# Grouped-query heads: the triangles of two key tiles share one block up to its transposing, and masks part them before the product with the values

## The chip, the cores and the metric

The kernel runs on one core of a Trainium2 chip. The metric is device time in microseconds (us), of which a smaller value is better. The time before the change is 1879.26 us, the median of three runs (1879.20, 1879.26 and 1881.03). The engines are named as in the profile: PE is the matrix engine (PEld its weight loads), DVE the vector engine, ACT the scalar engine, POOL the GpSimd engine, and SP the engine that issues the DMAs.

## The reference

One block of a transformer, in float32, for 512 positions and a width of 2048: a norm, one input projection whose columns are split over three kinds of mixers (A: 8 heads of dilated attention, B: a convolution module, C: 16 heads of windowed attention), an output projection with its residual, a second norm and a gated feed-forward network. The change concerns C alone: 16 query heads of 64, which share 2 heads of keys and values, with a window of 128 and one learned sink for each head.

```python
# q, k: normalised per head; G = 8 query heads for one key head
s = jnp.einsum('nbqhgd,nbkhd->nbhgqk', qb, kb) * (hd ** -0.5)
dist = qpos[:, :, None] - kpos[:, None, :]
valid = (dist >= 0) & (dist <= max_dist) & (kpos[:, None, :] >= 0)      # max_dist = 127
s = jnp.where(valid[None, :, None, None], s, -jnp.inf)
m = jnp.maximum(jnp.max(s, axis=-1), sk)                                # sk: the sink
p = jnp.exp(s - m[..., None])
denom = jnp.sum(p, axis=-1) + jnp.exp(sk - m)
o = jnp.einsum('nbhgqk,nbkhd->nbqhgd', p, vb) / denom
```

The positions form four tiles of 128. Query q of a tile looks at keys 0 to q of its own tile and at keys q+1 to 127 of the tile ahead of it. So the keys that a query may see are two triangles, one in each of two key tiles, and the two triangles together are exactly one square of 128 by 128.

## The kernel before

All products of the projections are made in three parts, from float32 values that are split into a high part (fp32r) and the low remainder. The input projection `project()` goes through 30 column tiles of 128 columns; a column tile is 16 blocks of the width, and a block is three matmuls of 512 columns (L312, L313, L314). After every second block, so after six projection matmuls, `project()` calls `ticks.tick()` (L486). The class `Ticks` (L91) holds a list of steps for each tick: `ticks.after(n, step, ...)` puts a step n ticks ahead, and `tick()` issues what has come due. So the attention steps stand in the instruction streams between groups of six projection matmuls, at places that whole numbers set, and each engine goes through its own stream in that order. The queue is not rearranged by times.

Heads are worked in pairs: a tile of the query projection (cq0 to cq7, worked in the order cq0 cq3 cq1 cq5 cq2 cq7 cq4 cq6) holds two heads. In the names of tiles, c5t is the bank of transposes of tile cq5, and so on; c5s, c5e, c5ph, c5pl and c5o are its scores, its exps, the high and the low part of the transposed weights, and its product with the values. `attention()` queues the steps of one head (`head(h)`), with the distances of the table `C_TICKS` (L43). For a C head they are:

- `scores` (two units, two ticks apart): for query tiles 0 and 1, then 2 and 3, the product of queries with the keys of the own tile and of the tile ahead, 256 columns (for tile 0: 128). PE writes the bank c5s (L736, L738, L739).
- `top`: DVE adds the mask `bias_c` to the scores and takes the maximum of each row (L750), and makes nm, the negative maximum times the row's scale.
- `exps`: ACT makes the exps with their sums: 128 columns for query tile 0, and 256 for each of the others (L763). Masked entries come out as zero.
- `norm`: DVE adds the sink's share and makes the reciprocal, and POOL scales the exps by it (L779), in the same widths: 128 and three times 256.
- `flip`: PE transposes the blocks of 128 by 128 (L795): seven of them for a head, two each for query tiles 1 to 3 and one for tile 0. They lie in two banks by `TBANKS` (L708): four blocks, and three blocks one tick later.
- `high` and `low`, for each bank: ACT casts the transposed block to fp32r (c5ph, L801), and a tick later DVE makes the remainder (c5pl, L806).
- `weigh`: PE multiplies the values with the transposed weights: eight matmuls (L819, L820), high and low in turn, since a key tile serves the query tile of its own and the one behind it: six of 256 columns and two of 128.
- `out_high` and `out_rows`: ACT and DVE gather the result in mix_c5 (L828); its split into mh_c and ml_c (ml_c on POOL, L865) feeds the output projection.

The second head of a pair runs six ticks behind the first, by the table's `every`. The products of the first head are in the same tick as the first transposes of the second.

All buffers of 128 x 512 come from one pool of 67 slots (`slot()`, L145), the banks of PSUM from `bank()`. The mixer A has eight heads with the same steps, but another table (`A_TICKS`); B works on DVE, with 30 taps for each of four tiles (L513), between the same projections.

Of the kernel before, what the change touches and what calls it, by code (L numbers as in the profile page):

```python
# [15 lines left out]
P = 128  # L16
T = 512
# [25 lines left out]
C_TICKS = (1, 6, 2, 2, 2, 2, 4, 1, 3)  # L43
# [79 lines left out]
def kernel(ctx: ExitStack, tc: tile.TileContext, xT, wi, wo, wgu, wd, cst_in, outT):  # L123
# [254 lines left out]
    bias_c = slot("bias_c", cols=2 * P)  # L378
# [5 lines left out]
    nc.gpsimd.iota(di2[:, :2 * P], pattern=[[-1, 2 * P]], base=P, channel_multiplier=1)  # L384
# [294 lines left out]
    def do_v(box, b, name):  # L679
# [29 lines left out]
        "c": [[(0, 0, 1), (1, 1, 2)], [(2, 2, 3), (3, 3, 3)]],  # L709
# [5 lines left out]
    def attention(kind, box, mix, mi, heads):  # L715
# [3 lines left out]
        mask = bias_c if kind == "c" else bias_a  # L719
        mw = mask.shape[-1]  # L720
        st = {}

        def head(h):
# [17 lines left out]
            def top(u):  # L741
                b, rq = banks[u], box["rq"]
                s = slice(us[u][0][0], us[u][-1][0] + 1)
                if kind == "c" and u == 0:
                    with_kl = slot(f"kl{h}", F32, P)
                    nc.scalar.copy(with_kl, b[:, P:2 * P])
                    nc.vector.tensor_add(with_kl, with_kl, mask[:, mw - P:])
                for i, k0, n, o in reversed(us[u]):
                    other = with_kl if kind == "c" and i == 0 else mask[:, mw - n:]
# [7 lines left out]
            def exps(u):  # L757
                b, rq = banks.pop(u), box["rq"]
                e = es[u] = slot(f"{name}e{h}{u}")
                s = slice(us[u][0][0], us[u][-1][0] + 1)  # L760
                for i, k0, n, o in us[u]:
                    acc = dict(accum_out=den[:, i:i + 1]) if kind == "c" else {}
                    nc.scalar.activation(e[:, o:o + n], b[:, o:o + n], AF.Exp, bias=nm[:, i:i + 1],  # L763
                                         scale=rq[:, i, h:h + 1], **acc)
# [3 lines left out]
            def norm(u):  # L768
# [9 lines left out]
                for i, k0, n, o in us[u]:  # L778
                    nc.gpsimd.tensor_scalar(e[:, o:o + n], e[:, o:o + n], rd[:, i:i + 1], None, op0=ALU.mult)  # L779
# [3 lines left out]
            def block(i, j):  # L783
                for u, un in enumerate(us):
# [14 lines left out]
            def high(t, b, o):  # L799
                ph[t] = slot(f"{name}ph{h}{t}", F32R)  # L800
                nc.scalar.copy(ph[t][:, :o], b[:, :o])  # L801
                ticks.after(EV, low, t, b, o)

            def low(t, b, o):
                pl[t] = slot(f"{name}pl{h}{t}", F32R)
                nc.vector.tensor_sub(pl[t][:, :o], b[:, :o], ph[t][:, :o].bitcast(F32))  # L806

            def weigh():
                b = bank(f"{name}o{h}")
                vals = box["v"][h]  # L810
                first = True
                for t, tb in enumerate(TBANKS[kind]):
# [251 lines left out]
    m_hi = m_lo = r1b = mult_a = bias_a = bias_c = None  # L1064
# [471 lines left out]
```

## Time and profile before

| what | us |
|---|---|
| median of three runs | 1879.26 |
| span of the profiled execution | 1877.5 |
| matmuls of the input projection, start of the first to the last | 5 to 397 |
| transposes of the C heads, among them | 136 to 371 |
| matmuls of the output projection | 398 to 593 |
| matmuls of the feed-forward network, from | 593 |

The runs' time holds a little around the span of the profile. A line of a timeline reads: start, duration, engine, line of the kernel, operation, output and inputs by the program's names, and the shape; one line may stand for several instructions that follow each other (x3). A line of groups gives the count, the busy time and the mean of one in ns, and behind a second bar the idle time of the engine ahead of these instructions, with what ended it. "<-DVE c0pl" names the engine and the tile whose result ended a wait. All durations of the profile come from one execution.

### The profile page before, as it was taken

What the parts mean: (1) busy time and instruction counts of PE and PEld (TensorE: products, weight loads), DVE (VectorE), ACT (ScalarE), POOL (GpSimd) and SP (SyncE); (2) the same over time, 40 slices, a digit from 0 to 9 for tenths busy, and PEclk for the clock granted to TensorE, in tenths of its full rate; (3) what the DMA queues carried; (4) which work ended last, traced back from release to release, by engine and by line L of the source; (5) the groups of instructions that cost most, each with busy time, mean ns of one, the idle gap of its engine ahead of it and who ended that gap; (6) DMA issues with size and microseconds to landing.
All of it is one profiled execution on the core that took longest, in us unless ns stands there. A gap on an engine that the chain in (4) does not pass through costs nothing.

```text
span 1877.5 us, 28557 instructions
## 1 busy us (share of the span) xinstructions
PE 1871.7 (100%) x9848; PEld 1609.1 (86%) x9848; DVE 1454.1 (77%) x2376; ACT 1343.7 (72%) x1883; POOL 1217.0 (65%) x812
## 2 busy tenths in 40 slices
PE   9999999999999999999999999999999999999999
PEld 7888888888888888888888888888888888888888
DVE  7578999897679777777777777777777677778887
ACT  6246655553466887888878888888888887777675
POOL 5023444362155887778878877888787767766786
PEclk9999999999999999999999999999999999999999
DMA  7333233333342354443544445344455475578984
GB/s 271 122 109 102 81 105 102 121 107 138 113 146 89 114 178 142 163 163 132 184 134 164 162 137 181 132 166 160 145 175 196 151 237 185 196 253 283 311 241 124
DMA packets 157986, 301.09 MB, mean 160 GB/s; under 512 B 29968, under 2 KB 69008, under 8 KB 157840
## 3 DMA queue, kind: packets, MB, share of 16 engines
q1 hardware_dynamic: 157696, 299.25, 48.8%
q8 instruction: 78, 1.28, 0.3%
q14 instruction: 68, 0.56, 0.1%
q10 hardware_dynamic: 144, 0.01, 0.0%
HBM read 241.27 MB, written 50.33 MB: 155 GB/s over the span
## 4 chain that ended last, share of the span: by engine, by line
PE 96%; DVE 1%; issue 1%; ACT 1%; POOL 1%; DMA 0%; SPq 0%; DVEq 0%; POOLq 0%; ACTq 0%
PE out L1125 51%; PE out L1267 16%; PE o L313 3%; PE o L314 3%; PE o L312 3%; PE cq L312 1%; PE cq L313 1%; PE cq L314 1%; PE in L313 1%; PE ak L312 1%; PE bg L312 1%; PE ak L314 1%; PE ak L313 1%; PE bu L312 1%; PE bu L314 1%; PE bg L313 1%
## 5 line engine op out<-in xcount | busy, mean ns | idle before, releaser
L1125 PE MATMUL out<-h,wh 128*128 128x512 f32 x2464 | 588.4, 391 | 0.0
L1125 PEld LDWEIGHTS out<-h,wh 128*128 128x128 f32 x2464 | 452.7, 188 | 87.5
L1125 PEld LDWEIGHTS out<-h,wl 128*128 128x128 f32 x2464 | 316.2, 191 | 12.4 <-DVE wl L295 0.4
L1125 PE MATMUL out<-h,wl 128*128 128x256 f32 x2464 | 320.3, 283 | 0.2 <-DVE wl L295 0.2
L1267 PE MATMUL out<-wh,a 128*128 128x512 f32 x896 | 221.3, 389 | 0.0
L1267 PEld LDWEIGHTS out<-wh,a 128*128 128x128 f32 x896 | 168.2, 188 | 34.9
L289 ACT CAST wh<-w 128x1024 fp32r<-128x1024 f32 (+1 forms) x93 | 96.7, 1042 | 125.0 <-PE o L313 43.3
L290 DVE TENSOR_TENSOR wl<-w,wh 128x1024 fp32r<-128x1024 f32 (+1 forms) x93 | 117.2, 1262 | 46.7 <-ACT wh L289 45.7
L1267 PE MATMUL out<-wl,a 128*128 128x512 f32 x448 | 119.7, 389 | 0.0
L1267 PEld LDWEIGHTS out<-wl,a 128*128 128x128 f32 x448 | 84.1, 188 | 17.4
L513 DVE SCALAR_TENSOR_TENSOR y<-bu,cst,y 128x511 f32<-128x511 f32 (+14 forms) x120 | 90.3, 753 | 0.7
L1125 PE MATMUL out<-a,wh 128*128 128x512 f32 x330 | 80.1, 391 | 0.0
L1125 PEld LDWEIGHTS out<-a,wh 128*128 128x128 f32 x330 | 60.2, 188 | 11.4
L312 PE MATMUL o<-mh_c,wh 128*128 128x512 f32 x128 | 51.2, 400 | 0.0
L313 PE MATMUL o<-ml_c,wh 128*128 128x512 f32 x128 | 50.1, 392 | 0.4 <-POOL ml_c L865 0.3
L314 PE MATMUL o<-mh_c,wl 128*128 128x512 f32 x128 | 50.1, 391 | 0.0
L1312 DVE TENSOR_TENSOR Y<-Y,out 128x512 f32<-128x512 f32 x48 | 30.8, 683 | 19.0 <-PE out L1267 18.9
L1125 PEld LDWEIGHTS out<-a,wl 128*128 128x128 f32 x330 | 43.3, 191 | 2.2
L1125 PE MATMUL out<-a,wl 128*128 128x256 f32 x330 | 44.0, 283 | 0.0
L429 POOL TENSOR_TENSOR ssum<-ssum,sq 128x512 f32<-128x512 f32 x15 | 26.6, 1770 | 19.3 <-ACT sq L428 18.8
L312 PE MATMUL cq<-hh,wh 128*128 128x512 f32 x96 | 38.6, 402 | 0.0
L314 PE MATMUL cq<-hh,wl 128*128 128x512 f32 x96 | 37.5, 391 | 0.0
(3111 smaller groups left out, 5197.0 us busy)
## 6 DMA issues: line engine op xcount, KB each, us to landing
od<-a SPq DMA_DIRECT2D x140, 256.0 KB, 4.7
a<-od SPq DMA_DIRECT2D x140, 256.0 KB, 6.2
w<-in_wi SPq DMA_DIRECT2D x59, 512.0 KB, 3.6
w<-in_wo SPq DMA_DIRECT2D x32, 512.0 KB, 3.6
x<-in_xT SPq DMA_DIRECT2D x16, 256.0 KB, 6.7
xr<-in_xT SPq DMA_DIRECT2D x16, 256.0 KB, 3.8
x2d<-xr SPq DMA_DIRECT2D x16, 256.0 KB, 2.0
yd<-z SPq DMA_DIRECT2D x16, 256.0 KB, 5.5
```

The lines of the kernel that those rows point to most:

```text
L289: nc.scalar.copy(hi[:, :n], t[:, :n])
L290: eng.tensor_sub(lo[:, :n], t[:, :n], hi[:, :n].bitcast(F32))
L312: nc.tensor.matmul(out, wh, xh, start=start, stop=False)
L313: nc.tensor.matmul(out, wh, xl, start=False, stop=False)
L314: nc.tensor.matmul(out, wl, xh, start=False, stop=stop)
L429: eng.tensor_add(acc, acc, sq)
L513: nc.vector.scalar_tensor_tensor(yconv[j][:, i:], hconv[j][:, :T - i], c, yconv[j][:, i:], op0=ALU.mult, op1=ALU.add)
L1125: nc.tensor.matmul(out, lhs[:, s], rhs, start=begin, stop=last and low == flip[0] and x is xs[-1], skip_group_check=True)
L1267: nc.tensor.matmul(to[h], x[:, h * P:(h + 1) * P], v[:, j], start=sub == 0 and h not in started, stop=sub == 1 and n in (len(todo) - 1, le ...
L1312: nc.vector.tensor_add(t, t, b)
```

## The change

The scores are still made for both key tiles. Then one square is made of them: where a key's place in the tile is behind the query's (the table `earlier`), the score of the own tile is overwritten by that of the tile ahead (`copy_predicated`). From there on a head has four blocks instead of seven: maximum, exps, sums and transposes work on 128 columns for each query tile. The normalising scale is applied by ACT instead of POOL. After the transposing there is one bank, one cast and one subtraction of 512 columns. Then `triangles()` parts each block into its two key tiles on POOL, by products with a mask of zeros and ones (`keys_c`): four products for the high part and four for the low part of a head (three of 2 x 128 columns and one of 128 each), which write two slots each. The matmuls with the values are as many and as wide as before, but the four high ones come first and then the four low ones, and they stand one tick later: the table's last number goes from 3 to 5, and one bank less is counted. Query tile 0 still gets its mask by an addition (`bias_c`, now 128 columns). The masks need one `iota` of 512 instead of 256 columns and two more slots, which are held until the output projection.

```diff
-C_TICKS = (1, 6, 2, 2, 2, 2, 4, 1, 3)
+C_TICKS = (1, 6, 2, 2, 2, 2, 4, 1, 5)
...
-    bias_c = slot("bias_c", cols=2 * P)
+    bias_c = slot("bias_c", cols=P)
+    keys_c = slot("keys_c")
+    earlier = slot("earlier", I32)
...
-        nc.vector.tensor_copy(df[:, :2 * P], di2[:, :2 * P])
-        nc.vector.tensor_scalar(r[:, :2 * P], df[:, :2 * P], 127.0, None, op0=ALU.is_le)
-        nc.vector.scalar_tensor_tensor(r[:, :2 * P], df[:, :2 * P], 0.0, r[:, :2 * P], op0=ALU.is_ge, op1=ALU.mult)
-        nc.vector.tensor_scalar(bias_c, r[:, :2 * P], 0.0, BIG, op0=ALU.is_equal, op1=ALU.mult)
+        nc.vector.tensor_copy(df, di2)
+        nc.vector.tensor_scalar(keys_c[:, :2 * P], df[:, :2 * P], 0.0, None, op0=ALU.is_le)
+        nc.vector.tensor_scalar(keys_c[:, 2 * P:], df[:, :2 * P], 0.0, None, op0=ALU.is_gt)
+        nc.vector.tensor_scalar(bias_c, df[:, 3 * P:], 0.0, BIG, op0=ALU.is_lt, op1=ALU.mult)
+        nc.vector.tensor_scalar(earlier[:, :2 * P], df[:, :2 * P], 0.0, None, op0=ALU.is_lt)
...
-        "c": [[(0, 0, 1), (1, 1, 2)], [(2, 2, 3), (3, 3, 3)]],
+        "c": [[(i, i, i) for i in range(NT)]],
...
             def top(u):
...
+                if grouped:
+                    first = 1 - u
+                    pair = b.rearrange("p (i t k) -> p i t k", i=2, t=2)[:, first:]
+                    keys = earlier[:, :2 * P].rearrange("p (i k) -> p i k", i=2)[:, first:]
+                    nc.vector.copy_predicated(pair[:, :, 1], keys, pair[:, :, 0])
+                    nc.vector.tensor_reduce(mx[:, 2 * u + first:2 * u + 2], pair[:, :, 1],
+                                            axis=mybir.AxisListType.X, op=ALU.max)
                 for i, k0, n, o in reversed(us[u]):
-                    other = with_kl if kind == "c" and i == 0 else mask[:, mw - n:]
+                    if grouped and i:
+                        continue
+                    other = with_kl if grouped else bias_a[:, T - n:]
...
             def exps(u):
...
+                    if grouped:
+                        src, to = b[:, o + n - P:o + n], e[:, i * P:(i + 1) * P]
...
             def norm(u):
...
-                    nc.gpsimd.tensor_scalar(e[:, o:o + n], e[:, o:o + n], rd[:, i:i + 1], None, op0=ALU.mult)
+                    if grouped:
+                        own = e[:, i * P:(i + 1) * P]
+                        nc.scalar.activation(own, own, AF.Copy, scale=rd[:, i:i + 1])
+                    else:
+                        nc.gpsimd.tensor_scalar(e[:, o:o + n], e[:, o:o + n], rd[:, i:i + 1], None, op0=ALU.mult)
...
             def high(t, b, o):
                 ph[t] = slot(f"{name}ph{h}{t}", F32R)
                 nc.scalar.copy(ph[t][:, :o], b[:, :o])
-                ticks.after(EV, low, t, b, o)
-
-            def low(t, b, o):
+                ticks.after(EV, low, t, b, o, ph[t])
+                if grouped:
+                    triangles("h", ph)
+
+            def triangles(part, p):
+                full = p.pop(0)
+                for u in range(2):
+                    t = p[u] = slot(f"{name}p{part}{h}{u}", F32R)
+                    for k in range(2):
+                        n = 2 - (u and k)
+                        src = full[:, (2 * u + k) * P:(2 * u + k + n) * P].bitcast(F32)
+                        nc.gpsimd.tensor_mul(t.rearrange("p (i t k) -> p i t k", i=2, t=2)[:, :n, k],
+                                             src.rearrange("p (i k) -> p i k", k=P),
+                                             keys_c[:, 2 * k * P:(2 * k + n) * P].rearrange("p (i k) -> p i k", k=P))
+
+            def low(t, b, o, hi):
                 pl[t] = slot(f"{name}pl{h}{t}", F32R)
-                nc.vector.tensor_sub(pl[t][:, :o], b[:, :o], ph[t][:, :o].bitcast(F32))
+                nc.vector.tensor_sub(pl[t][:, :o], b[:, :o], hi[:, :o].bitcast(F32))
+                if grouped:
+                    triangles("l", pl)
 
             def weigh():
...
+                if grouped:
+                    for p in (ph, pl):
+                        for i in range(NT):
+                            n = 2 * P if i < NT - 1 else P
+                            nc.tensor.matmul(b[:, i * P:i * P + n], vals[:, i].rearrange("p a b -> p (a b)"),
+                                             p[i // 2][:, i % 2 * 2 * P:i % 2 * 2 * P + n], start=first,
+                                             stop=p is pl and i == NT - 1, skip_group_check=True)
+                            first = False
+                    ticks.after(1, out_high, b)
+                    return
```

Where the instructions stand shows best at the second head of tile cq5, inside the projection of cq7. In the names below, c5t10 and c5t11 are the banks of transposes of that head, c5e10 and c5e11 its exps (c5e10 alone after the change), c5o0 is the product of the first head with the values cv0, and c2s10 holds the first scores of tile cq2. PE before, the end of the products of the first head with what follows in the same tick:

```order
L819 MATMUL c5o0_2166<-c5ph01_2114,cv0_831 128x256
L820 MATMUL c5o0_2166<-c5pl01_2132,cv0_831 128x256
L819 MATMUL c5o0_2166<-c5ph01_2114,cv0_831 128x128
L820 MATMUL c5o0_2166<-c5pl01_2132,cv0_831 128x128
L795 MATMUL c5t10_2175<-ident_110,c5e10_2024 128x128 x3
L795 MATMUL c5t10_2175<-ident_110,c5e11_2069 128x128
```

The next tick of PE before, where the second bank of transposes stands:

```order
L312 MATMUL cq7_2119<-hh9_338,wh36_2032 128x512
L313 MATMUL cq7_2119<-hl9_339,wh36_2032 128x512
L314 MATMUL cq7_2119<-hh9_338,wl36_2033 128x512
L795 MATMUL c5t11_2205<-ident_110,c5e11_2069 128x128 x3
L312 MATMUL cq7_2119<-hh10_359,wh36_2032 128x512
L313 MATMUL cq7_2119<-hl10_360,wh36_2032 128x512
L314 MATMUL cq7_2119<-hh10_359,wl36_2033 128x512
```

PE after the change, both ticks:

```order
L314 MATMUL cq7_2152<-hh7_292,wl35_1974 128x512
L815 MATMUL c5t10_2198<-ident_110,c5e10_2052 128x128 x4
L738 MATMUL c2s10_2210<-ck01_1043,cq21_1810 128x256
L740 MATMUL c2s10_2210<-ckh1_1026,cq21_1810 128x256
L741 MATMUL c2s10_2210<-ckl1_1027,cq21_1810 128x256
L312 MATMUL cq7_2152<-hh8_313,wh36_2060 128x512
L313 MATMUL cq7_2152<-hl8_314,wh36_2060 128x512
L314 MATMUL cq7_2152<-hh8_313,wl36_2061 128x512
L312 MATMUL cq7_2152<-hh9_340,wh36_2060 128x512
L313 MATMUL cq7_2152<-hl9_341,wh36_2060 128x512
L314 MATMUL cq7_2152<-hh9_340,wl36_2061 128x512
L851 MATMUL c5o0_2227<-c5ph00_2113,cv0_834 128x256 x2
```

The transposes and the scores keep their tick; the three transposes of the second bank are gone, and the products of the first head have moved to the place where these stood, one tick on, the high ones at their head.

On POOL, at the end of tile cq3's work (c3e00 to c3e11 are its exps, cq1r is the root for the norm of the next tile cq1), before:

```order
L779 TENSOR_SCALAR c3e00_1319<-c3e00_1319,c3d0_1062 128x128
L779 TENSOR_SCALAR c3e00_1319<-c3e00_1319,c3d0_1062 128x256
L779 TENSOR_SCALAR c3e01_1369<-c3e01_1369,c3d0_1062 128x256 x2
L779 TENSOR_SCALAR c3e10_1441<-c3e10_1441,c3d1_1063 128x128
L779 TENSOR_SCALAR c3e10_1441<-c3e10_1441,c3d1_1063 128x256
L779 TENSOR_SCALAR c3e11_1481<-c3e11_1481,c3d1_1063 128x256 x2
L585 TENSOR_TENSOR cq1r_1612<-cq1v_1594,nhalf_106 128x8
```

And after:

```order
L833 TENSOR_TENSOR c3pl00_1539<-c3pl00_1537,keys_c_124 128x2x128 x2
L833 TENSOR_TENSOR c3pl01_1542<-c3pl00_1537,keys_c_124 128x2x128
L833 TENSOR_TENSOR c3pl01_1542<-c3pl00_1537,keys_c_124 128x128
L833 TENSOR_TENSOR c3ph10_1621<-c3ph10_1619,keys_c_124 128x2x128 x2
L833 TENSOR_TENSOR c3ph11_1624<-c3ph10_1619,keys_c_124 128x2x128
L833 TENSOR_TENSOR c3ph11_1624<-c3ph10_1619,keys_c_124 128x128
L588 TENSOR_TENSOR cq1r_1627<-cq1v_1600,nhalf_106 128x8
L833 TENSOR_TENSOR c3pl10_1653<-c3pl10_1651,keys_c_124 128x2x128 x2
L833 TENSOR_TENSOR c3pl11_1656<-c3pl10_1651,keys_c_124 128x2x128
L833 TENSOR_TENSOR c3pl11_1656<-c3pl10_1651,keys_c_124 128x128
```

Where the scaling of the exps stood, ahead of the transposes, POOL now has the products behind the cast (ph) and behind the subtraction (pl), and the root of the next tile stands between the high and the low products of the second head.

More of the change, by code (lines that the diff above doesn't have):

```diff
@@ L383 @@
     di2 = slot("di2", I32)
-    nc.gpsimd.iota(di2[:, :2 * P], pattern=[[-1, 2 * P]], base=P, channel_multiplier=1)
+    nc.gpsimd.iota(di2, pattern=[[0, NT], [-1, P]], base=0, channel_multiplier=1)
     def masks():
@@ L718, in attention @@
         us = UNITS[kind]
-        mask = bias_c if kind == "c" else bias_a
-        mw = mask.shape[-1]
+        grouped = kind == "c"
         st = {}
@@ L758, in exps @@
                 b, rq = banks.pop(u), box["rq"]
-                e = es[u] = slot(f"{name}e{h}{u}")
+                e = es[u] = es[0] if grouped and u else slot(f"{name}e{h}{u}")
                 s = slice(us[u][0][0], us[u][-1][0] + 1)
                 for i, k0, n, o in us[u]:
-                    acc = dict(accum_out=den[:, i:i + 1]) if kind == "c" else {}
-                    nc.scalar.activation(e[:, o:o + n], b[:, o:o + n], AF.Exp, bias=nm[:, i:i + 1],
-                                         scale=rq[:, i, h:h + 1], **acc)
+                    acc = dict(accum_out=den[:, i:i + 1]) if grouped else {}
+                    if grouped:
+                        src, to = b[:, o + n - P:o + n], e[:, i * P:(i + 1) * P]
+                    else:
+                        src, to = b[:, o:o + n], e[:, o:o + n]
+                    nc.scalar.activation(to, src, AF.Exp, bias=nm[:, i:i + 1], scale=rq[:, i, h:h + 1], **acc)
                 if kind == "c":
@@ L1063 @@
                 m_hi.pop(row), m_lo.pop(row)
-    m_hi = m_lo = r1b = mult_a = bias_a = bias_c = None
+    m_hi = m_lo = r1b = mult_a = bias_a = bias_c = keys_c = earlier = None
     r2b = cp.tile([P, 3 * TH], F32, name="r2b")
```

7 lines of the change are left out of this document (5 added, 2 removed).

## The prediction

> **What bounds the kernel now.** I read the page first: the busy times of the engines and the chain that ended last.
>
> ```profile
> span 1877.5 us, 28557 instructions
> PE 1871.7 (100%) x9848; PEld 1609.1 (86%) x9848; DVE 1454.1 (77%) x2376; ACT 1343.7 (72%) x1883; POOL 1217.0 (65%) x812
> PE 96%; DVE 1%; issue 1%; ACT 1%; POOL 1%; DMA 0%; SPq 0%; DVEq 0%; POOLq 0%; ACTq 0%
> ```
>
> TensorE is busy for the whole span and is 96% of the chain. So a matmul or transpose that goes is worth the time it holds PE, and work on another engine is worth nothing until PE waits for it. Next the waits of PE between 100 and 420 us, where the heads lie, and the busy times there.
>
> ```profile
> PE o L313 <- POOL ml_c L865: 0.3, 1, 0.3
> PE c0o L820 <- DVE c0pl L806: 0.2, 1, 0.2
> 100.00:400.00 300.00, 299.76 (x1561) 254.17 (x1560) 267.57 (x647) 172.47 (x373) 121.78 (x101) 1.00 0.35 105
> ```
>
> The window row gives PE, PEld, DVE, ACT and POOL, then the granted clock. In 300 us PE is idle for 0.24, all of it one wait of a head's product (c0o) for DVE's low part. DVE is 89% busy, ACT 57%, POOL 41%, the clock 1.00. The stage is bound by PE alone; DVE has the least room, and POOL, which gets the new work, the most.
>
> **The change, part by part.**
>
> *Three transposes less in each of 16 C heads (L795).* The page's mean of one instruction overlaps its neighbours, so I take starts from the timeline. This is the group of three that goes, between projection matmuls:
>
> ```profile
> 223.77 0.39 PE L314 MATMUL cq<-hh,wl 128*128 128x512 f32 x1
> 224.00 0.49 PE L795 MATMUL c5t<-ident,c5e 128*128 128x128 f32 x3
> 224.24 0.48 PE L312 MATMUL cq<-hh,wh 128*128 128x512 f32 x1
> 224.56 0.39 PE L313 MATMUL cq<-hl,wh 128*128 128x512 f32 x1
> ```
>
> Projection matmuls with nothing between start 0.227 apart (223.77 to 224.00 shows such a step). From 223.77 to 224.56 are two steps, 0.454; it took 0.79. The three transposes cost 0.34, and 16 x 0.34 = **5.4 us** go.
>
> *The weighing a tick later.* The eight products of 256 and 128 columns stay. Their tick moves from the one in which the next head's four transposes stand to the following one. Does a shared gap cost less than two gaps? First shared (products, four transposes and three scores), then transposes and scores without products, then products alone:
>
> ```profile
> 220.69 0.39 PE L314 MATMUL cq<-hh,wl 128*128 128x512 f32 x1
> 220.91 0.28 PE L819 MATMUL c5o<-c5ph,cv 128*128 128x256 f32 x1
> 221.80 0.62 PE L795 MATMUL c5t<-ident,c5e 128*128 128x128 f32 x4
> 222.18 0.36 PE L736 MATMUL c2s<-ck,cq 128*128 128x256 f32 x1
> 222.62 0.40 PE L312 MATMUL cq<-hh,wh 128*128 128x512 f32 x1
> 222.85 0.40 PE L313 MATMUL cq<-hl,wh 128*128 128x512 f32 x1
> ...
> 188.91 0.39 PE L314 MATMUL bu<-h,wl 128*128 128x512 f32 x1
> 189.14 0.60 PE L795 MATMUL c1t<-ident,c1e 128*128 128x128 f32 x4
> 189.93 0.40 PE L312 MATMUL bu<-hh,wh 128*128 128x512 f32 x1
> 190.16 0.40 PE L313 MATMUL bu<-hl,wh 128*128 128x512 f32 x1
> ...
> 309.64 0.39 PE L314 MATMUL bg<-hh,wl 128*128 128x512 f32 x1
> 309.87 0.28 PE L819 MATMUL c4o<-c4ph,cv 128*128 128x256 f32 x1
> 310.76 0.45 PE L312 MATMUL bg<-hh,wh 128*128 128x512 f32 x1
> 311.04 0.39 PE L313 MATMUL bg<-hl,wh 128*128 128x512 f32 x1
> ```
>
> The same subtraction gives 2.16 - 0.45 = 1.71 shared, 1.25 - 0.45 = 0.80, and 1.40 - 0.45 = 0.95. Apart they cost 1.75, so the split gives back 0.04 where it happens, in 11 heads by the order of instructions: 0.4 us. What is left is 5.4 - 0.4 = **5.0 us**.
>
> *The new products on POOL (triangles).* Each head gets six tensor_mul over 256 columns and two over 128, which is seven times x, with x the time of one over 256. In exchange POOL loses the scaling (three of 256 and one of 128). No row shows this very form. The nearest are a two-input product over 256 columns outside the stage, and the scaling inside it where DVE's taps run:
>
> ```profile
> L980 POOL TENSOR_TENSOR ta<-h 128x256 f32<-128x256 f32 x8 | 7.5, 936 | 41.9 <-ACT h L965 41.9
> L779 POOL TENSOR_SCALAR c4e<-c4e,c4d 128x256 f32<-128x256 f32 x6 | 7.6, 1278 | 2.0 <-PE aq0f L568 1.5 <-issue 0.5
> ```
>
> I take x = 0.93, the row of the same kind; 1.28 is the upper bound, and nothing excludes a value lower than 0.93. Seven are 6.5 us a head.
>
> They lie beside PE if they end before the weighing asks for them. The steps of one head now (transposes at 221.80 above), and those of the slowest head:
>
> ```profile
> 224.48 0.59 ACT L801 CAST c5ph<-c5t 128x512 fp32r<-128x512 f32 x1
> 228.11 0.67 DVE L806 TENSOR_TENSOR c5pl<-c5t,c5ph 128x512 fp32r<-128x512 f32 x1
> 231.66 0.28 PE L819 MATMUL c5o<-c5ph,cv 128*128 128x256 f32 x1
> ...
> 147.19 0.52 PE L795 MATMUL c0t<-ident,c0e 128*128 128x128 f32 x3
> 152.41 0.59 ACT L801 CAST c0ph<-c0t 128x512 fp32r<-128x512 f32 x1
> 155.25 0.68 DVE L806 TENSOR_TENSOR c0pl<-c0t,c0ph 128x512 fp32r<-128x512 f32 x1
> ```
>
> Call the first transpose T. In c5 the high part ends at T+3.3, the low part at T+7.0, and the weighing starts at T+9.9, six ticks later. A seventh tick is 9.9/6 = 1.6 more, and 0.3 of transposes goes: T+11.2. High products come first and the last low one is asked for some 0.7 into the group, at T+11.9. POOL works 3.5x on the high part from T+3.3 (ends T+6.5), then 3.5x on the low part from T+7.0 (ends T+10.2). That leaves 1.7 us. The condition is 3.3 + 7x < 11.9, x < 1.23; for a head whose high part ends at T+2, x < 1.41. In c0's second head the low part ends at T+8.7: 8.7 + 3.3 = T+12.0, a wait of 0.1, up to 0.4 with contention, in place of the 0.24 shown above. So the products cost PE nothing, or 0.4.
>
> Weighed against a rule: the Trainium skill, "SBUF — State Buffer", section "Who interferes with whom", says that a DVE instruction with two SBUF inputs and a GpSimd instruction exclude each other for the whole instruction. The trace first:
>
> ```profile
> 292.48 0.73 DVE L513 SCALAR_TENSOR_TENSOR y<-bu,cst,y 128x494 f32<-128x494 f32 x1
> 293.73 3.10 POOL L779 TENSOR_SCALAR c4e<-c4e,c4d 128x256 f32<-128x256 f32 x2 [1.54 <-PE aq0f L568]
> 295.95 0.95 DVE L513 SCALAR_TENSOR_TENSOR y<-bu,cst,y 128x493 f32<-128x493 f32 x1
> L779 POOL TENSOR_SCALAR c5e<-c5e,c5d 128x256 f32<-128x256 f32 x6 | 5.7, 956 | 0.5 <-DVE c5d L777 0.5
> ```
>
> Two scalings of c4 amid taps take 3.10 where two of c5's average take 1.91, 0.6 more each, and the tap under them takes 0.95 instead of 0.73. By the skill's rule every product of a head amid taps may wait out a whole tap, and the sum would be that of the last rival; by the rows such heads average 1.28, 0.3 above the others, and the sum stays. So the trace agrees that the two engines hold each other up, and shows it for some instructions, not for all.
>
> *Exps and scaling on ACT.* Exps of 256 become 128, and four scalings of 128 columns are new, for which a copy of that size is the nearest row:
>
> ```profile
> L746 ACT COPY kl<-c5s 128x128 f32<-128x128 f32 x2 | 0.5, 272 | 0.0
> ```
>
> Four times 0.27 is 1.1 us more a head; the second cast (384 columns) goes and three exps halve, so less than 1.1 is left, on an engine that is 57% busy. The transposes stand four ticks, some 6.5 us, behind the scaling, and that hides it: nothing. Uncovered it would be up to 1.1 a head. The high cast moves ahead of the copy of the weighed rows (mix_c), behind which it stands now.
>
> *DVE.* One subtraction instead of two, and reductions over half the columns against two copies: less in all, on the fullest engine. It speeds the low part and the taps; PE doesn't wait for either except at 158 us, so nothing, or the 0.24 there. The mask operations are a few of 256 and 128 columns, done once, far ahead of c0's transposes (147.19 above): nothing.
>
> *What waits behind POOL.* The root for the next tile's norm (cq1r, L585) now stands behind the four high products of c3's second head, up to 3.3 us, and DVE's nm of c1 waits with it. c1's scores are at 169 and its transposes at 189 (rows here and above), so it is hidden. ACT's first exp of a0 waits for a slot that c4's last products read, at most 6.5 us, with weight casts queued behind; these run ahead of PE, so I count nothing, and put the case that they don't into the second rival.
>
> *What is late next.* All that follows on PE comes up to 5 us sooner, while DMAs keep their issue and length. The first scores of c1 are nearest:
>
> ```profile
> 166.59 0.47 SPq L609 DMA_DIRECT2D cq<-cq1lo  x1
> DMA to landing us min/median/max: 2.2/2.3/3.8
> 169.18 0.36 PE L736 MATMUL c1s<-ck,cq 128*128 128x256 f32 x1
> ```
>
> 166.59 + 2.2 is 168.8, 0.4 before the scores. They would now come some 0.9 sooner, so 0 to 0.5 of wait. The out-projection's wait for ml_c (0.3) may grow or go. Upwards that makes 0.5 + 0.3 + 0.4 (c0's products) = 1.2, downwards 0.24 and ml_c's 0.3, about 0.5. I add 0.25 for all of it, since c1's place is the one that the rows make likely.
>
> **Sum.** 1877.5 - 5.0 + 0.25 = 1872.75. The runs' median is 1879.26, 1.8 above the profiled span, so **1874.5 us**.
>
> **The rivals.**
>
> *Forecast: PE's time falls by the transposes.* For it: PE has 0.24 us of idle time in the stage. By the bounds of the sum 1873.8 to 1875.5 (1877.5 - 5.0 + 1.8 with -0.5 and +1.2); if the split costs nothing (0.4) and the transposes' price, read from starts to 0.01 us, is 0.02 low (16 x 0.02 = 0.3), down to 1873.0. Chance 0.55.
>
> *The products, or ACT behind them, are late in some heads.* Where taps and products meet, x is near 1.28 and c5's limit is 1.23: 7 x 0.05 = 0.35 for such a head; heads whose high part is late as c0's (T+5.8) wait 5.8 + 7 x 1.28 - 11.9 = 2.9. One such and several of the first kind give 1 to 4 us: 1875.5 to 1878.8. Against it: the usual head has 1.7 us to spare. Chance 0.25.
>
> *Nothing moves.* The freed 5 us turn into waits for DMAs or for POOL further on, since PE only reaches the same gate sooner: 1878.8 to 1880. Against it: there is no wait in the stage but 0.24, so no gate is that close. Chance 0.07.
>
> *Slower: POOL becomes the bound.* If every product waits a whole tap, x = 0.93 + 0.73 = 1.66, and seven are 11.6 us where the next head of a tile comes six ticks, 9.9 us, later. Past x = 1.41 each head waits 7 x (x - 1.41): the gain of 0.31 a head is used up at x = 1.455, 0.2% is lost from x = 1.49, and at 1.66 it is 16 x 1.75 = 28 us, 1902. For it: the shown 3.10 for two, 1.55 each, past the limit. (It is the Trainium skill's rule on DVE and GpSimd, above, at its worst.) Against it: even the heads amid the taps average 1.28, and not all heads have taps beside them. Chance 0.13.
>
> **How the numbers follow.** A measurement of this kernel can tell 0.2%, 3.8 us, from no change; faster means below 1875.5, slower above 1883.0. Faster 0.55, same 0.25 + 0.07 = 0.32, slower 0.13. The range takes the first two cases, 1873.0 to 1878.8, with 0.2 left out above.
>
> **What would show it.** Right: groups of four transposes stay near 0.45, groups of three are gone, the weighing stands alone at 0.95, and PE waits for POOL's c?p tiles in all under 0.5 us. The products' mean over 256 columns decides: below 1.2 the forecast holds, above 1.45 the last rival does. Wrong would be a row of PE waiting on POOL in most heads, or scores of c1 waiting for their DMA by more than 0.5.

## The result and the profile after

The changed kernel takes 1940.49 us (median of 5 runs, 1939.78 to 1940.78) against 1879.39 us (5 runs, 1879.20 to 1881.03): the ratio is 1.0324, with a 95% interval from 1.0311 to 1.0336. It is 61 us slower, where 4.8 us faster was forecast. First the page of the changed kernel: its span, the busy times, and the chain that ended last.

```profile
span 1938.0 us, 28560 instructions
PE 1891.7 (98%) x9800; PEld 1620.7 (84%) x9800; DVE 1470.8 (76%) x2329; ACT 1349.7 (70%) x1931; POOL 1263.3 (65%) x876
PE 77%; DVE 6%; ACT 2%; issue 1%; POOL 0%; DMA 0%; SPq 0%; DVEq 0%; ACTq 0%; POOLq 0%
```

PE has 48 instructions less, as it should, and yet is busy for 20.0 us more (1891.7 against 1871.7), and idle for 46.3 us (1938.0 - 1891.7) where it was idle for 5.8. These two, 20.0 and 40.5, are the 60.5 us by which the spans differ. DVE was to lose work and has 16.7 us more. Now the waits of PE over the whole span (sum, times, longest), and the busy times between 100 and 400 us.

```profile
PE ak2t L632 <- ACT ak2wide L625: 5.4, 1, 5.4
PE ak0t L632 <- ACT ak0wide L625: 5.4, 1, 5.4
PE c1o L851 <- POOL c1pl L833: 4.3, 4, 2.1
PE a1s L741 <- DVE ak1l L655: 3.8, 1, 3.8
PE a0s L741 <- DVE ak0l L655: 3.8, 1, 3.8
PE c0o L851 <- POOL c0pl L833: 3.7, 4, 1.5
PE c5o L851 <- POOL c5pl L833: 3.4, 2, 2.8
PE c1s L738 <- DMA cq<-cq1lo: 3.1, 1, 3.1
PE c2t L815 <- ACT c2e L795: 1.9, 1, 1.9
...
100.00:400.00 300.00, 266.01 (x1256) 220.31 (x1255) 233.85 (x484) 147.46 (x357) 135.98 (x135) 0.94 0.28 83
```

There were two waits of this stage before, 0.5 us together. The new ones name three engines and a DMA, and more than half of the rows shown name tiles that the change doesn't touch (ak2wide, ak0l, cq1lo). In the window every engine but POOL works less than before in the same 300 us: DVE 233.85 instead of 267.57, ACT 147.46 instead of 172.47. No engine has become the bound by its work; they wait for each other. ACT's scaling shows how, by its rows in the groups of instructions (the last number is idle time of ACT ahead of them):

```profile
L795 ACT ACTIVATE c5e<-c5e,c5d 128x128 f32<-128x128 f32 x8 | 2.8, 395 | 12.9 <-DVE c5d L791 12.8
L795 ACT ACTIVATE c7e<-c7e,c7d 128x128 f32<-128x128 f32 x8 | 2.8, 394 | 12.7 <-DVE c7d L791 12.7
```

Over the eight tiles ACT stands still for 85.5 us ahead of L795, waiting for DVE's reciprocal (L791), to do 22 us of work. The timeline around 290 us shows what that does to tiles that have nothing to do with it:

```profile
279.08 0.58 ACT L873 COPY mix_c<-c2o 64x512 f32<-64x512 f32 x1
284.36 0.17 DVE L791 RECIPROCAL c7d<-c7d 128x2 f32<-128x2 f32 x1
284.62 0.69 ACT L795 ACTIVATE c7e<-c7e,c7d 128x128 f32<-128x128 f32 x2 [4.97 <-DVE c7d L791]
...
286.41 1.04 ACT L289 CAST wh<-w 128x1024 fp32r<-128x1024 f32 x1
287.35 0.60 ACT L576 ACTIVATE ak2sq<-ak2f 128x512 f32<-128x512 f32 x1
287.48 1.23 DVE L290 TENSOR_TENSOR wl<-w,wh 128x1024 fp32r<-128x1024 f32 x1 [2.95 <-ACT wh L289]
292.91 0.17 DVE L583 TENSOR_TENSOR ak2v<-ak2v,c 128x8 f32<-128x8 f32 x1
293.15 2.07 POOL L588 TENSOR_TENSOR ak2r<-ak2v,nhalf 128x8 f32<-128x8 f32 x1 [7.72 <-DVE ak2v L583]
295.55 0.62 ACT L625 COPY ak2wide<-ak2r 128x512 f32<-128x512 f32 x1
296.22 1.12 PE L632 MATMUL ak2t<-ident,ak2wide 128*128 128x128 f32 x4 [5.41 <-ACT ak2wide L625]
```

ACT is ready at 279.66 and stands in its queue until 284.62, since the reciprocal lies behind a tap and the work of another head in DVE's queue. The cast of the next weights (wh) stands behind it in ACT's queue. DVE runs into that cast and stands for 2.95 us itself, and with it everything that DVE has next: the sums of ak2, the next reciprocals. So the norm of the keys ak2 goes through ACT (ak2sq), DVE, POOL and ACT again (ak2wide), late at each, and PE stands for 5.41 us. Each engine waits in turn for the other's queue.

### The profile page after: what moved, and what is told of

Same layout as the page of the kernel before. It is cut to its first block, busy times and chain, and to the rows that moved or that the text cites. A ratio compares the mean times of both kernels' runs of the same rounds, so it can differ in the third digit from the quotient of the medians.

```text
span 1938.0 us, 28560 instructions
## 1 busy us (share of the span) xinstructions
PE 1891.7 (98%) x9800; PEld 1620.7 (84%) x9800; DVE 1470.8 (76%) x2329; ACT 1349.7 (70%) x1931; POOL 1263.3 (65%) x876
## 4 chain that ended last, share of the span: by engine, by line
PE 77%; DVE 6%; ACT 2%; issue 1%; POOL 0%; DMA 0%; SPq 0%; DVEq 0%; ACTq 0%; POOLq 0%
PE out L1170 49%; PE out L1312 16%; PE o L313 3%; PE o L314 3%; PE o L312 3%; DVE y L516 1%; DVE wl L290 1%; ACT wh L289 1%; DVE h L990 0%; PE ak L312 0%; PE ak L314 0%; PE ak L313 0%; POOL ml_c L910 0%; DVE mix_c L878 0%; PE bg L314 0%
## 5 line engine op out<-in xcount | busy, mean ns | idle before, releaser
L516 DVE SCALAR_TENSOR_TENSOR y<-bu,cst,y 128x511 f32<-128x511 f32 (+14 forms) x120 | 98.5, 821 | 0.9
L432 POOL TENSOR_TENSOR ssum<-ssum,sq 128x512 f32<-128x512 f32 x15 | 26.6, 1772 | 18.6 <-ACT sq L431 18.1
L313 PE MATMUL cq<-hl,wh 128*128 128x512 f32 x96 | 38.6, 402 | 0.0
```

Of the source, the lines that this page charges most:

```text
L313: nc.tensor.matmul(out, wh, xl, start=False, stop=False)
L432: eng.tensor_add(acc, acc, sq)
L516: nc.vector.scalar_tensor_tensor(yconv[j][:, i:], hconv[j][:, :T - i], c, yconv[j][:, i:], op0=ALU.mult, op1=ALU.add)
```

## The experiments

Two causes were suspected: (A) the scaling on ACT, which makes ACT wait for DVE where POOL waited before, and (B) the products on POOL. The runs are told in their order; each has the kernel before beside it on the same chip (1879.15 to 1879.52 us).

**e1: the scaling two ticks later**

```diff
             def norm(u):
...
+                if grouped:
+                    ticks.after(2, own_scale, u)
+                    return
                 for i, k0, n, o in us[u]:
-                    if grouped:
-                        own = e[:, i * P:(i + 1) * P]
-                        nc.scalar.activation(own, own, AF.Copy, scale=rd[:, i:i + 1])
...
+            def own_scale(u):
+                for i, k0, n, o in us[u]:
+                    own = es[0][:, i * P:(i + 1) * P]
+                    nc.scalar.activation(own, own, AF.Copy, scale=rd[:, i:i + 1])
```

> The changed kernel, with the four scalings on ACT as a step of their own two ticks later; same instructions, other place in ACT's stream. Theory A (ACT stands in its queue for DVE's reciprocal, and the casts of weights, exps and widenings behind it come late; DVE then waits for ACT in turn): ACT's wait at L795 falls from 85 us in all to under 20, the waits of PE for ak0wide and ak2wide (5.4 each) go, and the time comes down by 40 to 65 us, to 1875 to 1900. Theory B (the products on POOL are late by themselves): the scalings' place changes nothing, 1930 to 1945. Theory C (PE's clock is lower because of the new mixture of work): 1935 to 1942.

Measured: 1900.98 us, 1.0112 (1.0095 to 1.0129). Not one instruction was taken away, and 39.5 us of the 61 are gone. ACT's wait at the scaling falls from 85.5 to 4.1 us, and PE's for ak2wide is gone. B alone and C are refuted; but 21.5 us stay, a little more than A allowed for.

**e2: the scaling back on POOL**

```diff
-                        nc.scalar.activation(own, own, AF.Copy, scale=rd[:, i:i + 1])
+                        nc.gpsimd.tensor_scalar(own, own, rd[:, i:i + 1], None, op0=ALU.mult)
```

> The changed kernel, with the scaling put back on POOL (four of 128 columns a head). Theory A: ACT no longer waits for DVE; PE's waits for ACT go, 1875 to 1905, where what is left above 1875 is waits for POOL, which now has about 9 us of work a head. Theory B: POOL gets more work, so the waits for c?pl grow: above 1945.

Measured: 1904.04 us, 1.0130 (1.0115 to 1.0145). Here too the loss falls, to 24.6 us, and with more work on POOL, where B expected it to grow.

**e3: no products**

```diff
                 if grouped:
-                    triangles("h", ph)
+                    whole(ph)
...
+            def whole(p):
+                p[1] = p[0]
```

> The changed kernel without the products of triangles(): the eight matmuls read the undivided cast tiles, so POOL has nothing to do for a C head (the masking is left out, the output is another). Theory A: the waits of ACT for DVE stay, and with them most of the loss; only PE's waits for POOL (about 12 us) go: 1915 to 1935. Theory B: all of the loss goes, about 1873 to 1880.

Measured: 1916.73 us, 1.0196 (1.0175 to 1.0218), from two runs that lie 6.2 us apart (1913.61 and 1919.85): 23.8 us of the loss go with the products, and 37 stay. Reading A expected PE's waits for POOL to go, some 12 us; about twice that went, so the products cost more than PE's waits for them. e6 takes this up.

**e4: the kernel before with its scaling on ACT**

```diff
                 for i, k0, n, o in us[u]:
-                    nc.gpsimd.tensor_scalar(e[:, o:o + n], e[:, o:o + n], rd[:, i:i + 1], None, op0=ALU.mult)
+                    if kind == "c":
+                        nc.scalar.activation(e[:, o:o + n], e[:, o:o + n], AF.Copy, scale=rd[:, i:i + 1])
+                    else:
+                        nc.gpsimd.tensor_scalar(e[:, o:o + n], e[:, o:o + n], rd[:, i:i + 1], None, op0=ALU.mult)
```

> The kernel before with one edit: the scaling of the C heads' exps on ACT instead of POOL, at the same place in the program (128 and three times 256 columns). Theory A: the loss shows without triangles: 15 to 60 us slower, 1895 to 1940. Theory B: no product is there to be late, 1879 within 3.

Measured: 1926.91 us, 1.0250 (1.0230 to 1.0271). One edit of the change, put alone into the kernel before, costs 47 us. (Its scalings have 128 and 256 columns, so ACT works on them for 28.8 us, against 22.4 in the changed kernel.) Its waits, of ACT, DVE and PE:

```profile
ACT c7e L780 <- DVE c7d L777: 11.9, 4, 4.1
...
DVE wl L290 <- ACT wh L289: 66.5, 50, 4.2
...
PE c0o L823 <- DVE c0pl L809: 5.3, 4, 2.7
PE ak0t L629 <- ACT ak0wide L622: 4.3, 1, 4.3
```

The same ring as above without any triangle: ACT waits for the reciprocal (73.0 us over the eight tiles), DVE for the cast of the weights (45.7 us in the kernel before), PE for both. That shows cause A by itself.

**e5: both, the scaling later and no products**

The edits of e1 and e3 together.

> The scaling two ticks later on ACT as in e1, and no products of triangles() (the masking is left out, the eight matmuls read the undivided tiles). Theory A+P (the place of the scaling, and the products, are the whole loss): the sum of the prediction is reached, 1872 to 1877. If a third cause is at work (the other DVE and ACT edits, the clock): 1880 or more.

Measured: 1876.56 us, 0.9985 (0.9976 to 0.9995). This is within the range of the theory that there are only two causes. The four kernels make a square: with the products 1940.5 (scaling at once) and 1901.0 (later), without them 1916.7 and 1876.6. The place of the scaling is worth 39.5 or 40.2, the products 23.8 or 24.4: they add up, well within the 6 us between e3's two runs. Without both the sign is the forecast one, in a kernel that leaves out the masking.

**e6: products with one input**

```diff
-                        nc.gpsimd.tensor_mul(t.rearrange("p (i t k) -> p i t k", i=2, t=2)[:, :n, k],
-                                             src.rearrange("p (i k) -> p i k", k=P),
-                                             keys_c[:, 2 * k * P:(2 * k + n) * P].rearrange("p (i k) -> p i k", k=P))
+                        nc.gpsimd.tensor_scalar(t.rearrange("p (i t k) -> p i t k", i=2, t=2)[:, :n, k],
+                                                src.rearrange("p (i k) -> p i k", k=P), 1.0, None, op0=ALU.mult)
```

How do products on POOL, which end in time for the most part, cost 24 us? In e1 PE waits for them just once, for 0.3, and ACT twice, for 8.9 in all (a0e and a1e, which take over slots that the last products read).

> e1 with the products replaced by POOL's tensor_scalar by 1.0 of the same shapes and outputs (one input instead of two; the masking is left out). Theory P1 (POOL's products hold up DVE's instructions that run beside them, and DVE has no room): what counts is how much DVE is slowed; if the second input matters, DVE's busy time falls from 1474.6 towards 1450 and the time to 1880 to 1890; if not, both stay as in e1, 1474 and 1900. Theory P2 (POOL's results and slots come late, DVE is not the reason): follows POOL's duration alone, so DVE's busy time falls and the time stays within 3 of e1's 1901, unless POOL gets shorter.

Measured: 1882.36 us, 1.0013 (1.0003 to 1.0022). Busy times and the taps of e1, from its page:

```profile
PE 1874.6 (99%) x9800; PEld 1610.0 (85%) x9800; DVE 1474.6 (78%) x2329; ACT 1350.2 (71%) x1931; POOL 1269.5 (67%) x876
L516 DVE SCALAR_TENSOR_TENSOR y<-bu,cst,y 128x511 f32<-128x511 f32 (+14 forms) x120 | 101.3, 844 | 0.9
```

The same rows of e6:

```profile
PE 1869.2 (99%) x9800; PEld 1606.1 (85%) x9800; DVE 1451.1 (77%) x2329; ACT 1349.6 (72%) x1931; POOL 1271.1 (68%) x876
L516 DVE SCALAR_TENSOR_TENSOR y<-bu,cst,y 128x511 f32<-128x511 f32 (+14 forms) x120 | 92.8, 774 | 0.9
```

And of e5, where POOL does none of this:

```profile
PE 1867.3 (100%) x9800; PEld 1605.1 (86%) x9800; DVE 1443.3 (77%) x2329; ACT 1350.1 (72%) x1931; POOL 1153.7 (62%) x748
L516 DVE SCALAR_TENSOR_TENSOR y<-bu,cst,y 128x511 f32<-128x511 f32 (+14 forms) x120 | 88.9, 741 | 0.9
```

DVE's instructions are the same in the three, 2329 of them. With products of two inputs beside them they take 31.3 us longer than with none, with one input 7.8. POOL is as busy in e6 as in e1. ACT's waits for POOL's products are 4.9 us in e6, with about the same durations on POOL. So the time isn't lost on POOL itself, but on DVE, which is held up beside the products of two inputs, and which was 89% busy in this stage (266.31 of the 300 us from 100 to 400 in e1). A place in e1's timeline shows it:

```profile
217.46 0.15 DVE L786 TENSOR_TENSOR c5d<-c5d 128x2 f32<-128x2 f32 x1
217.59 3.41 POOL L837 TENSOR_TENSOR c5ph<-c5ph,keys_c 128x256 fp32r<-128x256 f32 x4 [1.85 <-ACT c5ph L825]
217.72 2.27 DVE L516 SCALAR_TENSOR_TENSOR y<-bu,cst,y 128x491 f32<-128x491 f32 x2
219.91 0.70 DVE L786 TENSOR_TENSOR c5d<-c5d 128x2 f32<-128x2 f32 x1
```

Two taps take 2.27 us instead of 1.48 (twice e5's mean of 0.74), and an addition over two columns 0.70 beside the products, 0.15 just ahead of them. That addition is the step to the reciprocal for which ACT waits.

**e7: the parting on DVE, the scaling on POOL**

```diff
-                        nc.scalar.activation(own, own, AF.Copy, scale=rd[:, i:i + 1])
+                        nc.gpsimd.tensor_scalar(own, own, rd[:, i:i + 1], None, op0=ALU.mult)
...
-                ticks.after(ev, high, t, b, o)
+                ticks.after(ev, part_first if grouped else high, t, b, o)
...
+            def part_first(t, b, o):
+                for u in range(2):
+                    w = slot(f"{name}w{h}{u}")
+                    for k in range(2):
+                        n = 2 - (u and k)
+                        nc.vector.tensor_mul(w.rearrange("p (i t k) -> p i t k", i=2, t=2)[:, :n, k],
+                                             b[:, (2 * u + k) * P:(2 * u + k + n) * P].rearrange("p (i k) -> p i k", k=P),
+                                             keys_c[:, 2 * k * P:(2 * k + n) * P].rearrange("p (i k) -> p i k", k=P))
+                    ticks.after(1, high, u, w, 4 * P - u * P)
```

> The changed kernel, with the parting on DVE: four products of masks with the transposed bank itself, then two casts on ACT and two subtractions on DVE (three tiles' worth of work as before the change), and the scaling on POOL. So POOL has 4 instructions of 128 columns for a head and ACT waits for nobody new. Theory P1: DVE gets about 1.7 us of work a head for 1.6 of hold-up that goes, so it is as full as in e1: 1885 to 1905. Theory P2: with POOL out of the way, 1873 to 1880.

Measured: 1893.46 us, 1.0071 (1.0056 to 1.0086), with DVE busy for 1468.6. It falls into P1's range. With POOL out of the way, but the work on DVE, 13.9 of the 21.5 us stay: this fits the reading that DVE's time counts, whether it is spent on work or on being held up. The runs so far in which ACT doesn't scale right behind the reciprocal agree. Against the kernel before (1454.1) DVE is busy for 14.5 us more in e7 and the loss is 13.9; in e1 these are 20.5 and 21.5, in e2 21.7 and 24.6. In e6 DVE is busy for 3.0 us less, and 2.8 us are lost.

**e8: the exps a tick later**

```diff
-C_TICKS = (1, 6, 2, 2, 2, 2, 4, 1, 5)
+C_TICKS = (1, 6, 2, 2, 3, 2, 4, 1, 5)
```

This is on top of e1.

> e1 with the exps one tick later behind the maxima (the table's fifth number 2 to 3). If what is left in e1 is ACT standing in its queue for DVE (nm at L766: 47 us of idle time on ACT over the eight tiles), one more tick takes most of these waits and the time falls to 1880 to 1892; if DVE simply has too much work, the waits move elsewhere and the time stays at 1896 to 1905.

Measured: 1897.63 us, 1.0099 (1.0082 to 1.0115): 3.4 us from e1, so the second reading. ACT's waits at the exps fall from 48.6 to 8.4 us, and those at the scaling grow from 4.1 to 20.1. So ACT's waits nearly halve and the time hardly moves, while DVE is busy for 1471.5 us: here too the loss, 18.1 us, is close to DVE's 17.4 us above the kernel before.

**e9, e10, e11: triangles from positions**

On top of e1, e9 makes the triangles with an instruction that needs no mask as an input:

```diff
-                        nc.gpsimd.tensor_mul(t.rearrange("p (i t k) -> p i t k", i=2, t=2)[:, :n, k],
-                                             src.rearrange("p (i k) -> p i k", k=P),
-                                             keys_c[:, 2 * k * P:(2 * k + n) * P].rearrange("p (i k) -> p i k", k=P))
+                        sign = 1 - 2 * k
+                        nc.gpsimd.affine_select(out=t.rearrange("p (i t k) -> p i t k", i=2, t=2)[:, :n, k],
+                                                in_=src.rearrange("p (i k) -> p i k", k=P),
+                                                pattern=[[0, n], [sign, P]], base=-k, channel_multiplier=-sign,
+                                                compare_op=ALU.is_ge, fill=0.0)
```

e10 adds the table of e8 to it, and e11 to that a scaling one tick behind the reciprocal instead of two.

> e1 (the scaling two ticks later on ACT) with the parting by POOL's affine_select, which makes the triangles from the positions and so reads one input instead of two; what is computed is the reference's again. By the reading of e6 (it is the second input that holds DVE up): DVE's busy time near 1451, the time 1878 to 1885. If e6 was fast because it masked nothing and not because of its one input (other values, other waits): 1895 to 1903 as e1.

> e9 with the exps one tick later behind the maxima (fifth number 3), which took 3 us from e1: 1875 to 1882. If the waits of ACT for DVE no longer matter once DVE has room: the same as e9 within 1.5.

> e10 with the scaling one tick behind the reciprocal instead of two. The wait of c5t for c5e (3.4 in e6), which came from the scaling standing behind a table load and a wait for bg on ACT, goes: 1 to 3 below e10. If one tick is too short for DVE's reciprocal, ACT's waits at the scaling grow from under 5 us in all to over 20, and the time is 2 to 10 above e10.

Measured: e9 1879.86 us, 1.0000 (0.9991 to 1.0009); e10 1879.06, 0.9999 (0.9990 to 1.0008); e11 1879.98, 1.0004 (0.9995 to 1.0013). e9 decides what e6 left open: with the full result and one input the time is that of the kernel before. (This instruction is also shorter on POOL, 0.50 to 0.78 us by the groups' means over 256 columns, where the products of e1 take 0.87 to 1.25; e6, with one input and e1's durations, shows that this isn't what counts.) Its busy times, and one of its groups on POOL:

```profile
PE 1867.4 (99%) x9800; PEld 1605.0 (86%) x9800; DVE 1449.8 (77%) x2329; ACT 1349.5 (72%) x1931; POOL 1228.3 (65%) x876
...
L838 POOL TENSOR_SCALAR_AFFINE_SELECT c5pl<-c5pl 128x256 fp32r<-128x256 f32 x6 | 4.5, 775 | 3.9 <-DVE c5pl L845 3.9
```

DVE is at 1449.8, near e6's 1451.1. e10 and e11 can't be told from e9 or from each other: e10 ends the wait of c5t for c5e (2.4 us in e9), and new waits of 1 us each come elsewhere (ak1wide, and the DMA of cq7lo). For e11 neither reading came true. ACT's waits at the scaling do grow to 23.1 us, as the second reading said, but the time is only 0.9 above e10, where 2 to 10 was expected. So 23 us of such waits cost next to nothing here, where 85.5 us of them went with a loss of 39.5 in the changed kernel: ACT's waits are not a price by themselves, and how many of them reach PE was not measured apart.

**e12: e9 with the weighing on its old tick**

```diff
-C_TICKS = (1, 6, 2, 2, 2, 2, 4, 1, 5)
+C_TICKS = (1, 6, 2, 2, 2, 2, 4, 1, 4)
...
-                    ticks.after(2, own_scale, u)
+                    ticks.after(1, own_scale, u)
```

> e9 with the scaling one tick behind the reciprocal, and the weighing back on the tick of the kernel before (last number 4), so that it shares its gap with the next transposes again. PE's own time falls by another 0.4, the last ml_c comes a tick earlier, and c5t's wait of 2.4 goes: 1875 to 1878, the first kernel with all its work that is faster than before. If the parted tiles come too late for that tick (affine_select took 0.62 to 0.78 for 256 columns in e9, seven are 4.3 to 5.5 us): waits of PE for c0pl and others of 1 to 6 us in all, 1879 to 1885.

Measured: 1875.45 us, 0.9981 (0.9972 to 0.9990). This kernel computes everything and is faster than both: 3.7 us (0.2%, clear of the interval) less than the kernel before, 65 less than the changed one. Its span and the waits of PE from 100 to 420 us:

```profile
span 1873.8 us, 28572 instructions
PE c0o L857 <- POOL c0pl L838: 1.1, 1, 1.1
PE c3o L857 <- POOL c3pl L838: 0.3, 1, 0.3
PE o L313 <- POOL ml_c L916: 0.3, 1, 0.3
```

The earlier weighing costs the 1.1 of c0's second head, whose high part was known to be late. Which of its two edits gives how much of the 4.4 us to e9 was not separated.

## Why the prediction was wrong

**What bounds the kernel, and the gain on PE's own time, held.** PE's groups cost what was read from the kernel before. The weighing alone, in the changed kernel:

```profile
191.17 0.40 PE L314 MATMUL cq<-hh,wl 128*128 128x512 f32 x1
191.41 0.57 PE L851 MATMUL c3o<-c3ph,cv 128*128 128x256 f32 x4
191.82 0.64 PE L851 MATMUL c3o<-c3pl,cv 128*128 128x256 f32 x4
192.29 0.44 PE L312 MATMUL cq<-hh,wh 128*128 128x512 f32 x1
192.57 0.39 PE L313 MATMUL cq<-hl,wh 128*128 128x512 f32 x1
```

1.40 - 0.45 = 0.95, as predicted. The three transposes show only in the sum. In e5, where both causes are taken away, PE is busy for 4.4 us less than before (1867.3 against 1871.7; 5.0 was the sum), and 1.4 of it goes into waits: the span is 3.0 shorter.

**"The transposes stand four ticks ... behind the scaling, and that hides it: nothing."** This step failed, and it holds the larger part. It asked how long the scaling takes (1.1 us a head; the rows of the changed kernel say 1.4, eight in 2.8) and when its result is needed. It didn't ask what the instruction waits for itself, and what then stands behind it. On POOL the scaling waited for DVE's reciprocal as well (14.2 us for c0e, 8.9 for c3e in the kernel before). What stood behind it there, the next scalings, the roots for the norms of the next tiles and a product for B (bu), was not late for PE. On ACT the casts of the weights, the exps and the copies and squares of the other norms stand behind it. The prediction had this question for POOL ("What waits behind POOL"), and did not put it to ACT. e1 and e4 show the price: 39.5 us are gained by moving the scaling two ticks on, 47 us are lost by making this one edit alone.

**"The products cost PE nothing, or 0.4."** POOL's durations were sized well. Over 256 columns the groups' means lie between these two, around the 0.93 taken and below the limit of 1.23:

```profile
L833 POOL TENSOR_TENSOR c3ph<-c3ph,keys_c 128x256 fp32r<-128x256 f32 x6 | 6.7, 1140 | 5.8 <-ACT c3ph L821 5.8
L833 POOL TENSOR_TENSOR c7ph<-c7ph,keys_c 128x256 fp32r<-128x256 f32 x6 | 4.6, 788 | 6.4 <-ACT c7ph L821 6.4
```

PE's waits for them in the changed kernel are 12.0 us in all, and 0.3 in e1, where the scaling alone is moved; so these waits came with the first cause. The prediction had named this mean as what decides: below 1.2 the forecast holds. It stayed below, and the time rose by 61 us; the sign tested a step that was right. The other two signs of being wrong did show: 12.0 us of waits for these tiles instead of under 0.5, and 3.1 us of wait of c1's scores for their DMA.

**"DVE ... less in all ... so nothing."** This was the second step that failed. That DVE's own work falls is right: without the products, in e5, it is busy for 10.8 us less than before (1443.3 against 1454.1). The row of a tap beside POOL (0.95 instead of 0.73) was quoted, and used only for what POOL loses by it. The other side, what DVE loses, was left out of the sum, on the engine that had 11% of room. The runs put it at 31.3 us of DVE's time (e1 against e5), and at 21 to 24 us of the kernel's (e1 against e9 and e5).

A rule that was weighed there: the Trainium skill, "SBUF — State Buffer", section "Who interferes with whom", has a DVE instruction with two SBUF inputs and a GpSimd instruction that reads SBUF exclude each other, and leaves it to the order of issue which one blocks. The runs agree that DVE can be the one that is held up (0.15 to 0.70 for the addition over two columns). Three forms on POOL were run here, and they differ in degree by what POOL reads: with one input 7.8 and 6.5 us are lost (e6, e9), with two 31.3, which that section does not set apart.

**The rivals.** The last one had the sign, a place on POOL, and 1902 as its time. Its mechanism, POOL's products longer than a head has room for, was not what happened: by the groups' means x never passed 1.2 in the changed kernel. So its sign came out right by luck. **The late waits that were counted as small or as nothing** did come: 3.1 us for the DMA of cq1lo, where 0 to 0.5 was allowed, and 4.1 us of ACT's exps of a0 for c4's products. In e5, without both causes, PE has no wait for cq1lo.

## What to carry to other kernels

When an instruction is moved to another engine, ask first what it waits for, and list what stands behind it in its new queue; its duration and its result's due time are the smaller question. Where the producer's engine is nearly full, distance between producer and consumer in program order can be worth a lot: here the same instructions two ticks later gave back 39.5 of 61 us. And when an idle engine is given work, look at what it does to a nearly full neighbour: here a form with one input (a triangle made from positions instead of a mask) cost DVE 6.5 us instead of 31.3.

## What the hardware showed that was not expected

A wait of PE cost more than its length in this kernel. These are windows of the changed kernel around the wait of 5.41 us that ended at 296.22; the number behind POOL's is the clock granted to PE.

```profile
290.00:296.00 6.00, 0.81 (x5) 0.37 (x3) 5.08 (x16) 4.21 (x12) 2.07 (x1) 0.91 0.20 79
296.00:298.00 2.00, 1.78 (x7) 1.59 (x8) 1.96 (x3) 0.17 (x1) 0.00 (x0) 0.50 0.10 16
298.00:300.00 2.00, 2.00 (x6) 1.61 (x5) 0.62 (x3) 1.25 (x5) 0.00 (x0) 0.50 0.70 246
300.00:302.00 2.00, 2.00 (x6) 1.50 (x6) 0.92 (x2) 1.50 (x5) 0.42 (x1) 0.57 0.00 0
302.00:304.00 2.00, 2.00 (x12) 1.72 (x11) 1.94 (x3) 0.00 (x0) 2.00 (x4) 1.00 0.84 178
```

For some 5 us behind the wait the clock is 0.50, and the projection matmuls start 0.43 us apart (298.41, 298.84, 299.27) instead of 0.23. This accounts for PE being busier by 20.0 us with fewer instructions. Its own work fell by 4.4 us (e5), so slower matmuls cost about 24 us; and a mean clock of 0.988 over the span of 1938.0 us is some 23 us lost, while it is 1.000 in e5, e9 and e12. The Trainium skill, "TensorE: Matmul & The Clock Gate", section "Part 1: The HAM clock gate", gives half the clock after an idle window of about 3.4 us; the wait above agrees. But shorter waits did it as well: behind 1.53 and 0.60 us of idle time at c0o (they ended at 149.80 and 150.90), with a clock of 1.00 up to there, the next windows have

```profile
151.00:153.00 2.00, 2.00 (x7) 1.67 (x8) 2.00 (x3) 0.36 (x1) 0.00 (x0) 0.63 0.00 0
153.00:155.00 2.00, 2.00 (x8) 1.71 (x8) 1.97 (x4) 1.65 (x4) 1.28 (x1) 0.51 0.73 262
```

so no single wait of that length was needed here. How much idle time within how long a stretch is enough, these runs do not settle.
